# Forgetting attention: where in the unit loop the output projection's weight pieces are split

## The chip, the cores and the metric

The kernel runs on one core of a Trainium2 chip. The metric is the device time of one execution in microseconds (us). TensorE (PE) multiplies matrices, VectorE (DVE) and ScalarE (ACT) work on tiles element by element, GpSimd (POOL) does a smaller share of such work and issues some DMAs, and SyncE (SP) issues most DMAs. Each engine works through its own instructions in the order in which the program hands them out, and instructions of different engines wait for each other through semaphores.

## What is computed

A trunk of two layers over x (1 x 512 x 1024, fp32): a dilated-window attention layer with a gated convolution FFN, then a layer of forgetting attention, which shares one set of keys, values and cumulative gates c, with another FFN. The change lies in the forgetting attention:

```python
def fox_mixer(xn, w_q, w_o, k, v, c):
    q = (xn @ w_q).reshape(B, T, B_HEADS, HEAD_DIM)          # 16 heads of 64
    for i in range(T // BLK):                                # 4 blocks of 128 queries
        s = jnp.einsum('bqhd,bkhd->bhqk', q[:, q0:q1], k[:, :q1]) * scale
        s = s + (c_t[:, :, q0:q1, None] - c_t[:, :, None, :q1])
        p = jax.nn.softmax(jnp.where(causal, s, NEG), axis=-1)
        outs.append(jnp.einsum('bhqk,bkhd->bqhd', p, v[:, :q1]))
    return jnp.concatenate(outs, axis=1).reshape(B, T, B_WIDTH) @ w_o
```

## The kernel before

fp32 products are made of three matmuls. Each operand is split into a high part, rounded to the type that PE reads, and a low part that holds the rest; high by high, high by low and low by high are added up. So every weight is handled in pieces of 128 x 1024 by the class `Weights`, which has three steps for one piece:

- a load from HBM into a raw tile (L50, queue SP), made some pieces ahead: `high` of one piece also loads the piece behind the next one, since `ahead_dma` is 1 in this stage;
- `W.high()`: a copy on ACT that makes the high part (L60);
- `W.low()`: a subtraction on DVE, raw minus high (L78). In another form, `W.minus()` writes the negated and rounded raw tile with ACT (L71) and `W.low_added()` lets a DMA of POOL's queue add the raw tile to the result (L98); that form takes no DVE time.

The attention runs over 32 units (j, i): pair j of heads (0 to 7) and query block i (0 to 3). Unit (j, i) has (i + 1) * 128 keys. The loop hands out, for the unit at hand and its neighbours:

- on DVE `f_exp` (L1640), which adds the bias to the scores and finds the maximum, one instruction for each of two heads, then `f_norm` (L1652), which scales the probabilities of the unit before by the reciprocal of their sum;
- on ACT the exponentials of the unit (L1642), and copies of transposed probabilities out of PSUM (L1666);
- on POOL `f_bias` for the unit behind (L1612 and L1613);
- on PE the transposes of the probabilities of the unit two back (L1664); at i = 2 also the scores (L1630) of two blocks of this pair and two of the next, and the products with the values of the pair before (L1679, tile `o_ps`);
- `q_part` on PE (tile `q_ps`): queries of coming pairs, a quarter to a unit. The results are split by ACT at i = 0 (L1552) and by DVE at i = 1 (L1558).
- `f_out_high` and `f_out_low` (L1689 and L1693): the split of a pair's attention output, tile `OTb`.

The order is written out by hand (`manual_schedule`), so nothing is moved by a planner. All tiles of a kind come from one pool; PSUM has 8 banks, which scores, transposes and sums share.

The weight pieces that this stage splits are those of w_q_b (one for each pair) and then the eight of w_o_b, called wo0 to wo7 here. In pairs 2 to 5 one piece is split in each pair: high at the end of unit (j, 0), then negated and added by DMA at (j, 1). The last of these is wo0, in pair 5. From pair 6 on the DVE form is used, one piece to a unit: the highs of wo1, wo2 and wo3 stand at the end of units (6, 1), (6, 2) and (6, 3), and their lows in units (6, 2), (6, 3) and (7, 0), between `f_bias` and the transposes:

```python
            if i == 2 and j < 2 or (j, i) >= (6, 2):
                W.low()
```

In the last eight steps of the loop (from unit (6, 3) on) PE also gets `po.both(kc, b)`, six instructions of output projection for piece kc = 0 to 3 and row block b = 0, 1 (three for each half of 512 columns; tile `acc`). Behind the loop `po.finish` makes the rest of the first four pieces, and then those of wo4 to wo7; the first of these also splits the four pieces that remain and the first four of the next FFN (eight in a row on ACT and on DVE).

Of the kernel before, what the change touches and what calls it, by code (L numbers as in the profile page):

```python
# [117 lines left out]
def trunk_kernel(ctx, tc, x, norm_gains, w_qkv_a, w_o_a, w_q_b, w_o_b, kv_norm, w_kvf, b_f,  # L118
# [11 lines left out]
    def t8(shape, dt=F32, name="t8"):  # L130
        return p8.tile(shape, dt, tag="t8", name=name)
# [7 lines left out]
    def bank(shape, name="bank"):  # L139
        return psp.tile(shape, F32, tag="ps", name=name)  # L140
# [76 lines left out]
    W = Weights(nc, new_raw, lambda: t8([128, 2, 1024], F32R, name="w"), pieces)  # L217
# [64 lines left out]
    def mm3(o, ah, al, bh, bl, first, last, shared=False):  # L282
        pe.matmul(o, ah, bh, start=first, stop=False, skip_group_check=shared)  # L283
        pe.matmul(o, ah, bl, start=False, stop=False, skip_group_check=shared)  # L284
        pe.matmul(o, al, bh, start=False, stop=last, skip_group_check=shared)  # L285
# [90 lines left out]
    class Proj:  # L376
# [12 lines left out]
        def step(self, kc, b, hf):  # L389
            ah, al = self.get_act(kc)  # L390
            w = self.weight(kc)
            s = slice(b * 128, b * 128 + 128)
            if kc == 0:
                self.banks[b, hf] = bank([128, 512], name="acc")
            mm3(self.banks[b, hf], ah[:, s], al[:, s], w[0][:, H2[hf]], w[1][:, H2[hf]], kc == 0, kc == self.KC - 1)
# [1132 lines left out]
    def load_ck(j):  # L1528
        t = t4([128, 2, T], name="ck")
        s = cd[2 * j:2 * j + 2, :]  # L1530
        sp.dma_start(t, bass.AP(tensor=s.tensor, offset=s.offset, ap=[[0, 128], [T, 2], [1, T]]))
        cks[j] = t
# [4 lines left out]
    def q_part(j, i):  # L1537

        if j >= 8:
            return  # L1540
        if i == 0:
            qps[j] = (bank([128, T], name="q_ps"), [t.rearrange("p (k c) -> p k c", k=8) for t in W.get()])
        o, (wh, wl) = qps[j]
        for kc in (2 * i, 2 * i + 1):
            bh, bl = xs(xTq, kc, ALL)
            mm3(o, wh[:, kc, :], wl[:, kc, :], bh, bl, kc == 0, kc == KD - 1)

    def q_high(j):
        if j >= 8:
            return  # L1550
        qT[j] = t8([128, 2, T], F32R, name="qst")
        act.copy(qT[j][:, 0], qps[j][0])  # L1552

    def q_low(j):
        if j >= 8:
            return
        o, t = qps.pop(j)[0], qT[j]
        dve.tensor_tensor(t[:, 1], o, t[:, 0].bitcast(F32), ALU.subtract)  # L1558
# [48 lines left out]
    def f_bias(j, i):  # L1607
        n = (i + 1) * 128
        bias = t4([128, 2, T], name="bias")
        for hh in range(2):  # L1610
            hd = 2 * j + hh
            pool.tensor_scalar(bias[:, hh, :n], cks[j][:, hh, :n], -1.0, cq[:, i, hd:hd + 1], ALU.mult, ALU.add)  # L1612
        pool.affine_select(bias[:, :, n - 128:n], bias[:, :, n - 128:n], pattern=[[0, 2], [-1, 128]],  # L1613
                           compare_op=ALU.is_ge, fill=NEG, base=0, channel_multiplier=1)
        bia[j, i] = bias
# [3 lines left out]
    def f_scores(j, blocks):  # L1619
        wide = blocks[0] >= 2  # L1620
        if not wide:
            both = [bank([128, 2, 256], name="s_ps") for _ in range(2)]
        k = kst[j // 2][:, j % 2]
        for i in blocks:
            nn = max(256, (i + 1) * 128)
            sc[j, i] = [bank([128, T], name="s_ps") for _ in range(2)] if wide else [o[:, i] for o in both]
            for qp, kp in ((0, 0), (0, 1), (1, 0)):
                for hh in range(2):
                    own = slice(64 * hh, 64 * hh + 64)
                    pe.matmul(sc[j, i][hh][:, :nn], qT[j][own, qp, i * 128:(i + 1) * 128], k[own, kp, :nn],  # L1630
                              start=qp + kp == 0, stop=qp == 1)

    def f_exp(j, i):
        n = (i + 1) * 128
        s = sc.pop((j, i))
        bias = bia.pop((j, i))
        p = t4([128, 2, T], name="prob")
        nm, ls = small(2, "nm"), small(2, "ls")
        for hh in range(2):
            dve.tensor_tensor_reduce(p[:, hh, :n], s[hh][:, :n], bias[:, hh, :n], -0.125, BIG, ALU.add, ALU.min,  # L1640
                                     nm[:, hh:hh + 1])
            act.activation(p[:, hh, :n], p[:, hh, :n], AF.Exp, bias=nm[:, hh:hh + 1], scale=-1.0,  # L1642
                           accum_out=ls[:, hh:hh + 1])
        prob[j, i] = (p, ls)

    def f_norm(j, i):
        n = (i + 1) * 128
        p, ls = prob[j, i]
        rl = small(2, "rl")
        dve.reciprocal(rl, ls)  # L1650
        for hh in range(2):
            dve.tensor_scalar(p[:, hh, :n], p[:, hh, :n], rl[:, hh:hh + 1], None, ALU.mult)  # L1652
# [3 lines left out]
    def f_transpose(j, i):  # L1656
        p, _ = prob.pop((j, i))
        for hh in range(2):
            if i >= 2 or hh == 0:
                o = bank([128, 4, 128], name="pT_ps")  # L1660
                t = t2([128, 4, 128], name="pT")
            k0 = (i + 1) * hh if i < 2 else 0
            for k in range(i + 1):
                pe.transpose(o[:, k0 + k, :], p[:, hh, k * 128:(k + 1) * 128], ident)  # L1664
            if i >= 2 or hh == 1:
                act.copy(t[:, :k0 + i + 1], o[:, :k0 + i + 1])  # L1666
            pT[j, i, hh] = t[:, k0:k0 + i + 1]
# [16 lines left out]
    def f_out_high(j):  # L1684
        o = ops[j]
        if j % 2 == 0:
            OTb[j // 2] = t8([128, 2, 2, T], F32R, name=f"OTb{j // 2}")
        t = OTb[j // 2]
        act.copy(t[:, 0, j % 2, :], o)  # L1689

    def f_out_low(j):
        o, t = ops.pop(j), OTb[j // 2]
        dve.tensor_tensor(t[:, 1, j % 2, :], o, t[:, 0, j % 2, :].bitcast(F32), ALU.subtract)  # L1693

    units = [(j, i) for j in range(8) for i in range(4)]
    po = Proj(8, 4, lambda kc: (OTb[kc // 2][:, 0, kc % 2, :], OTb[kc // 2][:, 1, kc % 2, :]))
    wo = W.n_get + 7
    fill = [(kc, b) for b in range(2) for kc in range(4)]
    W.ahead, W.ahead_dma = 1, 1
    for i in range(3):  # L1700
# [9 lines left out]
    def values_of(n):  # L1710
        nonlocal pv_next
        while pv_next < n - 2:
            j, i = units[pv_next]
            pv_next += 1
            f_pv(j, i)
            if i == 3:
                outs.append(j)

    f_scores(0, (0, 1))
    for n in range(N + 3):  # L1720
        live = n < N
        if live:
            j, i = units[n]
            if i == 0 and j + 1 < 8:
                load_ck(j + 1)
            if i == 2:
                q_part(j + 2, 1)
                f_scores(j, (2, 3))
                if j + 1 < 8:
                    f_scores(j + 1, (0, 1))  # L1730
                values_of(n)
        if live:
            f_exp(j, i)
        if 1 <= n <= N:
            f_norm(*units[n - 1])
        if live:
            if n + 1 < N:
                f_bias(*units[n + 1])
            if i == 1:
                q_low(j + 1)  # L1740
            if i == 2 and j < 2 or (j, i) >= (6, 2):
                W.low()
            if i == 3 and j:
                f_out_low(j - 1)
            if i != 2:
                q_part(j + 1 + (i > 0), (i + 3) % 4)
            if (j, i) in ((7, 1), (7, 2)):
                next(down1)
        if 2 <= n < N + 2:
            f_transpose(*units[n - 2])  # L1750
        if live and i == 1 and 2 <= j < 6:
            W.minus()
            W.low_added()
        if n >= N + 3 - len(fill):
            po.both(*fill[n - N - 3 + len(fill)])

        if n >= N and n % 4 in (0, 2):
            values_of(n)
        while outs:
            f_out_high(outs.pop())  # L1760
        if live and i == 0:
            q_high(j + 1)
        if live and (i == (j < 2) if j < 6 else (j, i) >= (6, 1) and W.n_split < wo + 4):
            W.high()

    for _ in range(2):
        next(down1)
# [50 lines left out]
```

## Time and profile before

| | |
|---|---|
| median of 3 runs | 1107.76 us (1107.25 to 1108.35) |
| the profiled execution: its time | 1107.3 us |
| its span in the trace | 1105.5 us |
| granted TensorE clock | 0.999 |
| the stretch of the unit loop that is changed | about 686 to 726 us |

Times in the views are microseconds from the start of the span. A row of a timeline has the start, the duration, the engine, the line of the kernel, the operation, what it writes and reads, how many equal instructions are merged in the row, and in square brackets the idle time before it with what ended it. Where rows are merged the duration goes from the first start to the last end. PE's ends are modelled: matmuls overlap, and the step from one start to the next tells how fast they go.

### The profile page before, as it was taken

How to read it: one execution, taken by the hardware profiler on the slowest of the kernel's cores; microseconds unless marked ns; L12 is line 12 of the kernel's file. 1: busy time of each engine (PE TensorE's matmuls, PEld its weight loads, DVE VectorE, ACT ScalarE, POOL GpSimd, SP SyncE). 2: the span in 40 equal slices, each digit the busy share in tenths (PEclk: the TensorE clock that was granted, in tenths of full speed). 3: DMA queues.
4: the chain of work that ended last, by engine and by line, in shares of the span. 5: the costliest groups of instructions: out<-in, count | busy, mean ns of one | idle time of the engine just before them, and what ended most of it. 6: DMA issues, size and time to landing. Idle time of an engine off the chain costs nothing.

```text
span 1105.5 us, 18058 instructions
## 1 busy us (share of the span) xinstructions
PE 1095.3 (99%) x6609; PEld 951.4 (86%) x6609; DVE 878.3 (79%) x1493; ACT 672.3 (61%) x1116; POOL 213.3 (19%) x309
## 2 busy tenths in 40 slices
PE   9999999999999999999999999999999999999997
PEld 6988889899999988888878788789899999988886
DVE  6697788888788689897686677868888788779894
ACT  7654575756666747576451587746656666647572
POOL 2632001311111211000000546500311111211000
PEclk9999999999999999999999999999999999999999
DMA  9799854477987989794447434684368878979862
GB/s 323 179 367 411 312 170 136 90 184 187 214 191 185 243 264 324 287 322 116 133 153 274 172 108 123 187 267 128 84 179 202 203 186 186 235 265 325 311 248 76
DMA packets 184928, 236.26 MB, mean 214 GB/s; under 512 B 12352, under 2 KB 132152, under 8 KB 184840
## 3 DMA queue, kind: packets, MB, share of 16 engines
q1 hardware_dynamic: 169224, 182.94, 50.9%
q0 software_dynamic: 14944, 52.18, 20.6%
q8 instruction: 52, 0.85, 0.3%
q14 instruction: 36, 0.29, 0.1%
q10 hardware_dynamic: 672, 0.00, 0.0%
HBM read 166.08 MB, written 39.63 MB: 186 GB/s over the span
## 4 chain that ended last, share of the span: by engine, by line
PE 94%; ACT 2%; DVE 1%; DMA 1%; issue 1%; POOL 0%; SPq 0%; DVEq 0%; ACTq 0%; POOLq 0%
PE up L284 13%; PE up L283 13%; PE up L285 13%; PE acc L283 9%; PE acc L285 8%; PE acc L284 8%; PE v_ps L283 2%; PE v_ps L285 2%; PE v_ps L284 2%; PE qk_ps L284 2%; PE qk_ps L283 2%; PE qk_ps L285 2%; PE first L285 1%; PE first L283 1%; PE first L284 1%; PE k_ps L285 1%
## 5 line engine op out<-in xcount | busy, mean ns | idle before, releaser
L283 PE MATMUL acc<-w 128*128 128x512 f32 (+1 forms) x311 | 120.6, 388 | 0.3 <-DVE mix L332 0.3
L285 PE MATMUL acc<-w 128*128 128x512 f32 (+1 forms) x311 | 120.4, 387 | 0.0
L284 PE MATMUL acc<-w 128*128 128x512 f32 (+1 forms) x267 | 103.2, 387 | 0.0
L283 PE MATMUL up<-xsh,w 128*128 128x256 f32 x352 | 99.6, 283 | 0.0
L284 PE MATMUL up<-xsl,w 128*128 128x256 f32 x352 | 99.6, 283 | 0.0
L285 PE MATMUL up<-xsh,w 128*128 128x256 f32 x352 | 99.6, 283 | 0.0
L78 DVE TENSOR_TENSOR w<-wraw,w 128x1024 fp32r<-128x1024 f32 x62 | 82.0, 1339 | 21.6 <-ACT w L60 21.2
L620 ACT ACTIVATE bb<-up,conv 128x512 f32<-128x512 f32 x80 | 59.6, 776 | 58.7 <-DVE up L1007 47.9
L60 ACT CAST w<-wraw 128x1024 fp32r<-128x1024 f32 x82 | 84.3, 1048 | 17.1 <-PE v_ps L284 6.9
L284 PE MATMUL up<-xcl,w 128*128 128x512 f32 (+1 forms) x276 | 93.5, 339 | 0.0
L284 PE MATMUL up<-xbl,w 128*128 128x512 f32 (+1 forms) x276 | 93.5, 339 | 0.0
L283 PE MATMUL up<-xbh,w 128*128 128x512 f32 (+1 forms) x276 | 93.5, 339 | 0.0
L283 PE MATMUL up<-xch,w 128*128 128x512 f32 (+1 forms) x276 | 93.5, 339 | 0.0
L285 PE MATMUL up<-xbh,w 128*128 128x512 f32 (+1 forms) x276 | 93.5, 339 | 0.0
L285 PE MATMUL up<-xch,w 128*128 128x512 f32 (+1 forms) x276 | 93.4, 338 | 0.0
L283 PEld LDWEIGHTS acc<-w 128*128 128x128 f32 x311 | 58.4, 188 | 12.4 <-DVE mix L332 0.7
L285 PEld LDWEIGHTS acc<-w 128*128 128x128 f32 x311 | 58.4, 188 | 12.0
L283 PEld LDWEIGHTS up<-xsh,w 128*128 128x128 f32 x352 | 67.6, 192 | 0.0
L284 PEld LDWEIGHTS up<-xsl,w 128*128 128x128 f32 x352 | 67.6, 192 | 0.0
L285 PEld LDWEIGHTS up<-xsh,w 128*128 128x128 f32 x352 | 67.6, 192 | 0.0
L621 DVE SCALAR_TENSOR_TENSOR bb<-up,conv,bb 128x511 f32<-128x511 f32 x80 | 59.5, 743 | 5.5 <-ACT bb L620 5.5
L623 DVE SCALAR_TENSOR_TENSOR bb<-up,conv,bb 128x510 f32<-128x510 f32 x80 | 59.9, 748 | 2.8
(312 smaller groups left out, 3154.8 us busy)
## 6 DMA issues: line engine op xcount, KB each, us to landing
wraw<-in_w_up_dram SPq DMA_DIRECT2D x88, 512.0 KB, 5.7
w<-wraw POOLq DMA_DIRECT2D x32, 512.0 KB, 6.4
dT<-dsums SPq DMA_DIRECT2D x28, 512.0 KB, 6.6
w<-wsum POOLq DMA_DIRECT2D x24, 512.0 KB, 5.8
dsums<-in_w_down_dram SPq DMA_DIRECT2D x22, 512.0 KB, 7.5
dsums<-in_w_down_dram SPq DMA_DIRECT2D x44, 256.0 KB, 7.5
hD<-hc POOLq DMA_DIRECT2D x44, 256.0 KB, 6.4
dact<-hD SPq DMA_DIRECT2D x44, 256.0 KB, 5.4
```

The costliest lines, as they stand in the source:

```text
L60: self.nc.scalar.copy(pair[:, 0], raw)
L78: self.nc.vector.tensor_tensor(pair[:, 1], raw, pair[:, 0].bitcast(F32), ALU.subtract)
L283: pe.matmul(o, ah, bh, start=first, stop=False, skip_group_check=shared)
L284: pe.matmul(o, ah, bl, start=False, stop=False, skip_group_check=shared)
L285: pe.matmul(o, al, bh, start=False, stop=last, skip_group_check=shared)
L620: act.activation(bb[:, s, :], ps, AF.Identity, bias=cp[:, 3, ch:ch + 1], scale=cp[:, 2, ch:ch + 1])
L621: dve.scalar_tensor_tensor(bb[:, s, 1:], ps[:, :T - 1], cp[:, 1, ch:ch + 1], bb[:, s, 1:], ALU.mult, ALU.add)
L623: dve.scalar_tensor_tensor(bb[:, s, 2:], ps[:, :T - 2], cp[:, 0, ch:ch + 1], bb[:, s, 2:], ALU.mult, ALU.add)
```

## The change

The low of units (6, 2) and later in the middle of the loop body goes, and so does the rule that puts highs at the end of units from (6, 1) on. In their place a table names, for five units, steps at the very end of the loop body (behind `f_transpose`, `po.both`, `f_out_high` and `q_high`): wo1 is split at the end of (5, 1), behind the minus and the added DMA of wo0; the high of wo2 at the end of (6, 0), its low at the end of (6, 1) with high and low of wo3; wo4's high at the end of (7, 0) and its low at the end of (7, 1). One piece more, wo4, is split inside the loop, and one fewer behind it. Each high still issues one load on SP, so the loads move with the highs.

```diff
-    wo = W.n_get + 7
+    out_weights = {(5, 1): (W.high, W.low), (6, 0): (W.high,), (6, 1): (W.low, W.high, W.low), (7, 0): (W.high,),
+                   (7, 1): (W.low,)}
...
-            if i == 2 and j < 2 or (j, i) >= (6, 2):
+            if i == 2 and j < 2:
                 W.low()
...
-        if live and (i == (j < 2) if j < 6 else (j, i) >= (6, 1) and W.n_split < wo + 4):
+        if live and j < 6 and i == (j < 2):
             W.high()
+        if live:
+            for step in out_weights.get((j, i), ()):
+                step()
```

The order of instructions on each engine: on PE nothing moves. On DVE the subtractions of wo1 to wo3 go from behind the norms of (6, 1), (6, 2) and (6, 3) to in front of `f_exp` of (5, 2) (one) and of (6, 2) (two), and that of wo4 in front of `f_exp` of (7, 2). On ACT the copies go behind L71 of pair 5 (wo1), behind the query copy L1552 of (6, 0) (wo2), behind the copies of the transposes of (5, 3) (wo3, in the place where wo1 was) and behind those of (6, 2) (wo4).

## The prediction

> **What bounds the kernel now.** I read the busy shares first, then the windows around the unit loop's end, then PE's waits, then the timelines engine by engine.
>
> ```profile
> PE 1095.3 (99%) x6609; PEld 951.4 (86%) x6609; DVE 878.3 (79%) x1493; ACT 672.3 (61%) x1116; POOL 213.3 (19%) x309
> ```
>
> PE is busy 99% of the span, so time can come only from PE's few idle stretches, and a step moved elsewhere costs only what PE then waits for. The windows (start:end, length, then busy time and count of PE, PEld, DVE, ACT, POOL, then clock, DMA share, GB/s) show where those stretches are:
>
> ```profile
> 686.00:698.00 12.00, 11.96 (x112) 9.81 (x111) 9.16 (x30) 9.70 (x28) 8.37 (x15) 1.00 0.54 135
> 698.00:711.00 13.00, 11.61 (x106) 9.23 (x102) 11.80 (x34) 10.66 (x28) 9.74 (x14) 1.00 0.70 241
> 711.00:726.00 15.00, 15.00 (x139) 12.21 (x135) 10.70 (x26) 6.71 (x17) 2.22 (x4) 1.00 0.65 217
> 726.00:740.00 14.00, 14.00 (x62) 11.62 (x63) 9.26 (x10) 8.29 (x10) 0.00 (x0) 1.00 1.14 325
> ```
>
> Between 698 and 711 PE lacks 13.00 - 11.61 = 1.39 us; it lacks nothing from 711 to 740. The clock is 1.00 throughout. Of PE's waits over the whole span one group is of this place, and the timeline shows its largest, at (6,3)'s transposes:
>
> ```profile
> PE pT_ps L1664 <- DVE prob L1652: 1.4, 3, 1.1
> ...
> 701.65 0.88 PE L1664 MATMUL pT_ps<-ident,prob 128*128 128x128 f32 x6
> 703.75 0.82 PE L1664 MATMUL pT_ps<-ident,prob 128*128 128x128 f32 x6
> 707.03 0.66 PE L1664 MATMUL pT_ps<-ident,prob 128*128 128x128 f32 x4 [1.07 <-DVE prob L1652]
> 707.96 0.63 PE L1664 MATMUL pT_ps<-ident,prob 128*128 128x128 f32 x4 [0.27 <-ACT pT L1666]
> ```
>
> The transposes of a unit wait for DVE's norm (L1652) of that unit. From 698 to 711 DVE is busy 11.80 of 13.00 us, so DVE sets the pace there, just, and PE stands 1.07 and 0.27 us. This decides the case: lows on DVE are moved earlier, to (5,1) and (6,1), and the question is whether PE has work ahead while DVE does them.
>
> **The change part by part.** PE's instructions keep their order. "Late" below is against the traced execution.
>
> *wo1 at the end of (5,1).* Its high goes on ACT behind wo0's negated copy, its low on DVE ahead of `f_exp` of (5,2).
>
> ```profile
> 687.20 1.08 ACT L71 ACTIVATE w<-wraw 128x1024 fp32r<-128x1024 f32 x1
> 688.25 0.62 ACT L1642 ACTIVATE prob<-prob,nm 128x384 f32<-128x384 f32 x1
> 697.59 1.07 ACT L1666 COPY pT<-pT_ps 128x512 f32<-128x512 f32 x2
> 698.53 1.07 ACT L60 CAST w<-wraw 128x1024 fp32r<-128x1024 f32 x1
> 699.48 0.64 ACT L1642 ACTIVATE prob<-prob,nm 128x384 f32<-128x384 f32 x1
> ```
>
> ACT starts the negated copy (L71) at 687.20 and the next instruction 1.05 later. A high (L60) lasts 1.07 and takes 0.95 from start to next start (698.53 to 699.48). So wo1's high runs from about 688.2 to 689.25, and its low can't start before 689.25. DVE's rows here (L1640 is `f_exp`, first of two heads; L1652 is `f_norm`; L78 a low):
>
> ```profile
> 687.65 0.56 DVE L1640 CUSTOM_DVE_ANT_0 prob<-s_ps,bias 128x384 f32<-128x384 f32 x1 [2.08 <-PE s_ps L1630]
> 688.80 1.55 DVE L1652 TENSOR_SCALAR prob<-prob,rl 128x256 f32<-128x256 f32 x2
> 691.39 0.69 DVE L1640 CUSTOM_DVE_ANT_0 prob<-s_ps,bias 128x512 f32<-128x512 f32 x1 [1.05 <-POOL bias L1613]
> 694.84 1.28 DVE L1652 TENSOR_SCALAR prob<-prob,rl 128x512 f32<-128x512 f32 x2
> 698.28 0.54 DVE L1640 CUSTOM_DVE_ANT_0 prob<-s_ps,bias 128x384 f32<-128x384 f32 x1
> 699.42 0.66 DVE L1652 TENSOR_SCALAR prob<-prob,rl 128x256 f32<-128x256 f32 x2
> 700.00 1.20 DVE L78 TENSOR_TENSOR w<-wraw,w 128x1024 fp32r<-128x1024 f32 x1
> 701.12 0.68 DVE L1640 CUSTOM_DVE_ANT_0 prob<-s_ps,bias 128x512 f32<-128x512 f32 x1
> 703.96 1.23 DVE L78 TENSOR_TENSOR w<-wraw,w 128x1024 fp32r<-128x1024 f32 x1 [0.45 <-ACT w L60]
> 705.10 0.68 DVE L1693 TENSOR_TENSOR OTb<-o_ps,OTb 128x512 fp32r<-128x512 f32 x1
> 706.32 1.49 DVE L1652 TENSOR_SCALAR prob<-prob,rl 128x512 f32<-128x512 f32 x2
> 707.73 1.21 DVE L78 TENSOR_TENSOR w<-wraw,w 128x1024 fp32r<-128x1024 f32 x1
> ```
>
> A low costs DVE 1.12 (700.00 to the next start at 701.12). What lies beside it on POOL is the bias of (5,3):
>
> ```profile
> 689.19 1.69 POOL L1612 TENSOR_SCALAR bias<-ck,cq 128x512 f32<-128x512 f32 x2
> 696.90 1.46 POOL L1612 TENSOR_SCALAR bias<-ck,cq 128x512 f32<-128x512 f32 x2 [0.52 <-DVE rl L1650]
> 699.41 1.96 POOL L1612 TENSOR_SCALAR bias<-ck,cq 128x128 f32<-128x128 f32 x2 [0.56 <-DVE rl L1650]
> 706.68 2.75 POOL L1612 TENSOR_SCALAR bias<-ck,cq 128x512 f32<-128x512 f32 x2
> ```
>
> Norms and biases stretch each other: two biases of 512 columns took 1.46, 1.69 and 2.75 us, the norm of 256 columns 1.55 beside POOL's row at 689.19 and 0.66 at 699.42. So the bias that starts at 689.19, 0.06 before the low, may hold it off for one of its two instructions, 1.46 / 2 = 0.73. I take that: the low runs from 689.9, and `f_exp` of (5,2) starts at 691.0 in place of 687.65. In a sentence apart: the Trainium skill, "SBUF — State Buffer", section "Who interferes with whom", says of DVE in its two-port modes and GpSimd: "Whoever issues first gets the shared pair for the whole instruction; the other **fully blocks**"; the stretched rows agree that they collide, not that the block is whole, and by it the 0.06 us lead is what makes the difference between this sum and the first rival below.
>
> From `f_exp` to the norm behind it is 688.80 - 687.65 = 1.15; the norm of (5,1) costs 0.66 to 1.55, I take 1.0, as the bias is half done by then. So `f_exp` of (5,3) starts at 691.0 + 1.15 + 1.0 = 693.15, not 691.39: 1.75 late. The 3.35 us are cut to 1.75 by the 1.05 us for which DVE stood ahead of 691.39, and by the shorter norm. From there DVE runs without a gap to the norm of (5,3), whose end moves from 694.84 + 1.28 = 696.12 to 697.87. Who waits for that:
>
> ```profile
> 691.17 0.44 PE L1664 MATMUL pT_ps<-ident,prob 128*128 128x128 f32 x2
> 694.69 2.14 PE L1664 MATMUL pT_ps<-ident,prob 128*128 128x128 f32 x14
> 696.76 2.62 PE L1630 MATMUL s_ps<-kst,qst 64*128 64x384 f32 x24
> ```
>
> The transposes of (5,0) at 691.17 write a PSUM bank that the first scores of (5,2) leave when their `f_exp` has read them, now at 691.0 + 0.56: PE about 0.4 late. In the 14 transposes from 694.69 on, the last four belong to the second half of that norm, and the scores at 696.76 follow 0.64 behind its end: there PE already moves with DVE. So PE is then 1.75 late: a further +1.35.
>
> *wo2's high at (6,0), and low wo2, high and low wo3 at (6,1).* On ACT, wo2's high stands ahead of the exponentials of (6,1): 0.95 more before the copies (L1666) of (5,3)'s transposes. These start at 697.59 + 1.75 + 0.95 = 700.3 and wo3's high 0.94 behind them (698.53 - 697.59), from 701.2 to 702.3. Low wo2, ready long before, is over by then. Low wo3 waits for that high, and behind it on DVE is queued `f_exp` of (6,2), with the norm of (6,1): low wo3 from 702.3 to 703.4, `f_exp` at 703.4 in place of 698.28, norm of (6,1) from 703.4 + (699.42 - 698.28) = 704.55 to 705.2. PE's six transposes at 701.65 hold two of (6,0) and four of (6,1); the last two of these ran at about 702.0 and now wait until 705.2: PE is 3.2 late, +1.45 on the 1.75.
>
> Here too a load moves: wo3's, which SP now issues at (5,1), behind the ck load of pair 7.
>
> ```profile
> 690.91 0.33 SPq L1531 DMA_DIRECT2D ck<-cd  x1
> 694.81 6.75 SPq L50 DMA_DIRECT2D wraw<-in_w_o_b_dram  x3
> ...
> DMA to landing us min/median/max: 3.8/5.9/8.2
> ```
>
> At worst it is issued 1.5 us behind 690.91 (the bias of (5,3), late by one low and its wait, is what the ck load waits for) and lands 8.2 later, at 700.6, ahead of 701.2: no cost, with 0.6 us to spare. wo4's load likewise moves out of the three at 694.81 to earlier, with more to spare.
>
> *What is given back.* In (6,2) and (6,3) DVE no longer has its lows. From 701.12 to the end of the norm of (6,3), 706.32 + 1.49 = 707.81, were 6.69 us; of these low wo2 and its wait, from 703.96 - 0.45 = 703.51 to 705.10, 1.59, are gone. `f_exp` of (6,3) now starts at about 705.15, so that norm ends at 705.15 + 6.69 - 1.59 = 710.25: 2.45 late. PE's last four transposes of (6,3), at 707.96 before, then start at 710.4. PE came to them 3.2 late but loses its two stalls there: net -0.8. PE is 2.4 late, and no wait of PE's follows until 740 in the windows above.
>
> *wo4 in the loop, one piece fewer behind it.* The low that stood at 707.73 goes (-1.12 on DVE) and wo4's is added a unit later (+1.12): PE is full from 711 to 726 and DVE busy 10.70 of 15.00, which hides it; were the cover gone, 1.12. Behind the loop ACT and DVE are spared 0.95 and 1.12, but PE is busy 14.00 of 14.00 there: worth 0.
>
> Sum: 0.4 + 1.35 + 1.45 - 0.8 = **+2.4 us**. The profiled execution took 1107.3 us for a span of 1105.5, so it would take 1109.7; the median of the runs shown is 1107.76, 0.46 above it, and gives **1110.2**. Here 0.2% of the time, about what a measurement of this kernel can tell from no change, is 2.2 us.
>
> **The rivals.**
>
> *The low of wo1 gets in first.* If the low isn't held off (the 0.06 us are less than what my steps are known to), it starts at 689.25, DVE is 1.75 - 0.73 = 1.0 late in (5,3), and all that follows is 0.7 earlier: +1.7, so 1109.5. For it: the lows at 700.00 to 707.73 lasted 1.20 to 1.23 though POOL's rows beside them were stretched to 1.96 and 2.75, so it was POOL that gave way. Against: norms did stretch.
>
> *Not slower: DVE's tail is what bounds, and it is relieved.* The two stalls of (6,3) and their like go, and the steps moved to (5,1) and (6,1) find cover in PE's queue. If all 1.39 us between 698 and 711 go and nothing is added, 1107.76 - 1.39 = 1106.4. It decides at 691.39, where DVE stood 1.05 us idle: if `f_exp` of (5,3) is less than about 0.4 late there, and wo3's high is done before DVE comes to it, this is the outcome. For it: PE's idle time is at the tail alone. Against: L71 and L60 can't be done before 689.25, whatever DVE does. In a sentence apart: the Trainium skill, "Perfetto Trace Analysis", section "Identifying the Most-Contended Engine", has one improve the engine that is most occupied, by which moves on DVE and ACT beside a PE at 99% are worth about nothing, 1107.8; the 1.07 us stall shows that they are not hidden everywhere.
>
> *The port is fought over again at (6,1).* If the delayed norm of (6,1) meets a bias as the norm at 688.80 did, it takes 1.55, not 0.66: 0.9 on top of the chain that ends last, +3.3, so 1111.1. The same side is reached if wo3's load lands late, for each us beyond its 0.6. Against: POOL is busy for 9.74 of the 13.00 us there, so 3.26 are free of it.
>
> That the change doesn't do what it says is excluded by the instruction order: the pieces move to where the table puts them.
>
> **How the numbers follow.** The forecast gets 0.46, the low that gets in first 0.22, the second fight 0.18, not slower 0.14. The forecast's own range, from what the norm of (5,1) costs (0.66 to 1.55 about 1.0: -0.35 and +0.55) and the copies' shift, is 1109.4 to 1111.0. The whole range reaches down to 1106.8, over half of the not-slower case, and up to 1112.4, which leaves out 0.08 where fight and late load come together. Slower by over 2.2 us (above 1109.96): 0.6 of the forecast, 0.28, the second fight 0.18, and 0.02 of the first rival: 0.48. Faster by over 2.2 us needs more than the 1.39 us that PE lacks there: 0.06. The rest, 0.46, is within.
>
> **What would show it.** Right: L60 twice in a row from 687.2, `f_exp` of (5,2) at 691.0 with DVE idle time before its low put down to ACT or POOL; the norm of (5,3) ending near 697.9; new PE waits for DVE at (5,3) and (6,1); PE's stalls of 1.07 and 0.27 gone; the loop ending 2.4 us later. Wrong: `f_exp` of (5,3) within 0.4 us of 691.39; wo3's high before DVE has finished low wo2; or a change of time behind 726, where I have none.

## The result and the profile after

| 21 runs of each | median, us | range |
|---|---|---|
| before | 1107.85 | 1106.77 to 1111.13 |
| after | 1109.31 | 1107.95 to 1111.20 |

The ratio after to before is 1.0013, 95% interval 1.0007 to 1.0019: slower by 1.4 us (0.8 to 2.1). The prediction had +2.4 us; its first rival, in which the low of wo1 gets in first, had +1.7. Among the runs of the experiments further below, one execution of one kernel (lows in both gaps) took 1350.62 us at a granted clock of 0.752; its ratio leaves that one out.

The profiled execution of after took 1109.31 us, with a span of 1107.5. In the page, PE is as busy as before:

```profile
PE 1096.1 (99%) x6609; PEld 951.7 (86%) x6609; DVE 877.2 (79%) x1493; ACT 672.3 (61%) x1116; POOL 212.6 (19%) x309
```

To see where two executions part I matched the 6609 PE instructions of the two traces one by one and took how much later each starts. The median difference is 0.72 us just ahead of the first changed place, 1.41 behind the transposes of (5, 3), 3.39 in the middle of the six of (6, 2) (3.54 behind the last of them), 2.02 behind those of (6, 3), and 2.03 from 740 to 880 us. The first 0.7 us are not the change's: they arise near 387 us, where PE waits 0.8 us for a DMA that the kernel before shows no wait for, long ahead of the first instruction that moves. What the change does is 2.02 - 0.72 = 1.3 us in this pair of traces, in three steps: +0.7 at (5, 3), +2.0 at (6, 1) and (6, 2), -1.4 at (6, 3). PE's waits over the whole span of after (in total, times, longest):

```profile
PE pT_ps L1664 <- DVE prob L1652: 1.6, 3, 1.2
...
PE up L285 <- DMA w<-wsum: 0.8, 1, 0.8
PE pT_ps L1664 <- ACT prob L1642: 0.7, 1, 0.7
```

The same transposes in PE's timeline of after (start, duration, idle time before in brackets; about 0.7 of each start is that earlier offset). PE waits before (5, 3) and inside (6, 1), and the two stalls at (6, 3) are gone:

```profile
691.89 0.44 PE L1664 MATMUL pT_ps<-ident,prob 128*128 128x128 f32 x2
...
695.39 0.82 PE L1664 MATMUL pT_ps<-ident,prob 128*128 128x128 f32 x6
696.95 1.21 PE L1664 MATMUL pT_ps<-ident,prob 128*128 128x128 f32 x8 [0.74 <-ACT prob L1642]
698.10 2.70 PE L1630 MATMUL s_ps<-kst,qst 64*128 64x384 f32 x24
...
704.74 0.93 PE L1664 MATMUL pT_ps<-ident,prob 128*128 128x128 f32 x4 [1.24 <-DVE prob L1652]
...
706.98 1.14 PE L1664 MATMUL pT_ps<-ident,prob 128*128 128x128 f32 x6
...
709.34 1.25 PE L1664 MATMUL pT_ps<-ident,prob 128*128 128x128 f32 x8
```

The view puts the 0.74 us down to ACT's exponentials of (6, 0), which end at 696.91; the first half of DVE's norm of (5, 3) had ended only 0.1 us before. Both stand behind the late `f_exp` of (5, 3) on DVE.

DVE's rows at the two changed places, with ACT's highs and POOL's bias beside them:

```profile
687.87 1.08 ACT L71 ACTIVATE w<-wraw 128x1024 fp32r<-128x1024 f32 x1
688.83 1.05 ACT L60 CAST w<-wraw 128x1024 fp32r<-128x1024 f32 x1
...
700.91 1.06 ACT L60 CAST w<-wraw 128x1024 fp32r<-128x1024 f32 x1
```

```profile
689.91 1.23 DVE L78 TENSOR_TENSOR w<-wraw,w 128x1024 fp32r<-128x1024 f32 x1 [3.67 <-ACT w L60]
691.06 0.55 DVE L1640 CUSTOM_DVE_ANT_0 prob<-s_ps,bias 128x384 f32<-128x384 f32 x1
...
692.21 0.76 DVE L1652 TENSOR_SCALAR prob<-prob,rl 128x256 f32<-128x256 f32 x2
692.89 0.68 DVE L1640 CUSTOM_DVE_ANT_0 prob<-s_ps,bias 128x512 f32<-128x512 f32 x1
...
696.32 1.14 DVE L1652 TENSOR_SCALAR prob<-prob,rl 128x512 f32<-128x512 f32 x2
...
699.69 1.21 DVE L78 TENSOR_TENSOR w<-wraw,w 128x1024 fp32r<-128x1024 f32 x1
702.01 1.23 DVE L78 TENSOR_TENSOR w<-wraw,w 128x1024 fp32r<-128x1024 f32 x1 [1.11 <-ACT w L60]
703.15 0.55 DVE L1640 CUSTOM_DVE_ANT_0 prob<-s_ps,bias 128x384 f32<-128x384 f32 x1
...
704.30 0.88 DVE L1652 TENSOR_SCALAR prob<-prob,rl 128x256 f32<-128x256 f32 x2
705.10 0.67 DVE L1640 CUSTOM_DVE_ANT_0 prob<-s_ps,bias 128x512 f32<-128x512 f32 x1
...
708.63 1.24 DVE L1652 TENSOR_SCALAR prob<-prob,rl 128x512 f32<-128x512 f32 x2
```

```profile
689.87 2.47 POOL L1612 TENSOR_SCALAR bias<-ck,cq 128x512 f32<-128x512 f32 x2
```

At (5, 1), L60 starts 0.96 behind L71 and ends at 689.88; the low starts at 689.91, at once, and DVE's next instruction 1.15 later. So the low was not held off; POOL's two biases beside it took 2.47 us. At (6, 1) the second low waits 1.11 us for L60, and `f_exp` of (6, 2) stands behind it until 703.15, 2.3 us longer than behind the first low alone (699.69 and 1.15 for a low).

### The profile page after: what moved, and what is told of

It is laid out like the page before. It is cut to its first block, busy times and chain, and to the rows that moved or that the text cites. A ratio compares the mean times of both kernels' runs of the same rounds, so it can differ in the third digit from the quotient of the medians.

```text
span 1107.5 us, 18060 instructions
## 1 busy us (share of the span) xinstructions
PE 1096.1 (99%) x6609; PEld 951.7 (86%) x6609; DVE 877.2 (79%) x1493; ACT 672.3 (61%) x1116; POOL 212.6 (19%) x309
## 4 chain that ended last, share of the span: by engine, by line
PE 93%; DVE 2%; ACT 1%; DMA 1%; issue 1%; POOL 0%; DVEq 0%; ACTq 0%; POOLq 0%
PE up L285 12%; PE up L283 12%; PE up L284 12%; PE acc L283 9%; PE acc L285 8%; PE acc L284 8%; PE v_ps L283 2%; PE v_ps L285 2%; PE v_ps L284 2%; PE qk_ps L284 2%; PE qk_ps L285 2%; PE qk_ps L283 2%; PE first L285 1%; PE first L283 1%; PE first L284 1%; PE k_ps L285 1%
## 5 line engine op out<-in xcount | busy, mean ns | idle before, releaser
L60 ACT CAST w<-wraw 128x1024 fp32r<-128x1024 f32 x82 | 84.4, 1048 | 16.3 <-PE v_ps L284 6.9
```

Of the source, the lines that this page charges most:

```text
L60: self.nc.scalar.copy(pair[:, 0], raw)
```

## The experiments

All kernels were timed in several rounds on the same chip as runs of the kernel before. The intervals of their ratios are about 0.09% to each side, 1 us, as wide as what is looked for; so each profile was also matched with the trace of before, PE instruction by PE instruction. Differences in us, by place: (5, 3) is read behind the scores that follow its transposes, (6, 2) in the middle of its six transposes (behind the last of them a loss is 0.15 to 0.2 larger, and so is what (6, 3) then gives back), the last behind 712 us; "timed" is the ratio times 1107.8:

| kernel | (5, 3) | (6, 1), (6, 2) | (6, 3) | sum | ratio (95%) | timed |
|---|---|---|---|---|---|---|
| the change | +0.69 | +1.98 | -1.38 | +1.29 | 1.0013 (1.0007 to 1.0019) | +1.4 |
| first part | +0.71 | 0.00 | 0.00 | +0.72 | 1.0012 (1.0004 to 1.0021) | +1.3 |
| second part | +0.05 | +2.02 | -1.38 | +0.69 | 1.0002 (0.9993 to 1.0010) | +0.2 |
| wo1's low in (5, 2) | +0.56 | +2.03 | -1.39 | +1.19 | 1.0009 (1.0000 to 1.0018) | +1.0 |
| wo4 only | +0.18 | 0.00 | -0.41 | -0.23 | 0.9998 (0.9990 to 1.0007) | -0.2 |
| wo3's low in (6, 2) | +1.66 | +0.79 | -0.97 | +1.48 | 1.0007 (0.9998 to 1.0016) | +0.8 |
| one low behind norm (6, 3) | +0.30 | 0.00 | -0.73 | -0.43 | 0.9994 (0.9985 to 1.0003) | -0.7 |
| wo0's low in the gap | -0.74 | 0.00 | -0.67 | -1.41 | 0.9983 (0.9974 to 0.9992) | -1.9 |
| lows in both gaps | -0.71 | 0.00 | -1.52 | -2.22 | 0.9976 (0.9967 to 0.9985) | -2.7 |
| before, added DMA moved | +0.81 | 0.00 | +0.03 | +0.85 | 1.0005 (0.9996 to 1.0014) | +0.6 |
| change, added DMA moved | +0.37 | +1.96 | -1.38 | +0.95 | 1.0007 (0.9998 to 1.0016) | +0.8 |
| change, wo0 by DVE | +0.63 | +1.98 | -1.38 | +1.24 | 1.0008 (0.9999 to 1.0017) | +0.9 |

Where nothing was changed ahead of a place, the column shows how much one execution differs from another: up to 0.3 at (5, 3), 0.4 at (6, 3). In no kernel did PE's difference change by more than 0.05 between 712 and 880 us, so up to there none lost or won anything behind the loop. From 888 us on it grows by 0.1 to 0.4 us in four of them (in three at a wait for a weight DMA); the sums leave that out, and the changed kernel doesn't have it.

In the diffs below `out_weights` is the table of steps at the end of a unit. A second table stands in the old place of the lows, in the middle of the unit; it is added in all but the two kernels that move the added DMA:

```diff
-            if i == 2 and j < 2:
+            if i == 2 and j < 2 or (j, i) in out_lows:
                 W.low()
```

**The first part alone** (against the kernel after):

```diff
+    out_weights = {(5, 1): (W.high, W.low), (6, 2): (W.high,), (6, 3): (W.high,)}
+    out_lows = ((6, 3), (7, 0))
```

> Only the first part of the change: wo1 is split at the end of (5, 1), wo2 and wo3 keep the places that they had (highs at the end of (6, 2) and (6, 3), lows in (6, 3) and (7, 0)), and wo4 stays behind the loop. Theory (late norms: each moved low holds up the softmax of the next unit, and PE pays where it has nothing queued): PE is 0.8 us late from the transposes of (5, 3) on, as in the changed kernel; the low that is gone from (6, 2) gives nothing back, since the low in (6, 3) waits for its high on ACT instead (that wait grows from 0.45 to about 1.5 us), so +0.8 at the end, 1108.6. Rival (occupied DVE: a low costs 1.12 us of a DVE that paces PE from 698 to 711, wherever it stands): +0.8 at (5, 3), but the stall of 1.07 at (6, 3) goes, so -0.3, 1107.6. Rival (loads and pieces: the loss comes from wo4 and the moved loads): 0.0.

+0.7 at (5, 3), and nothing given back, as the first theory had it. DVE's rows show why one low less in (6, 2) is worth nothing: DVE reaches the next low early and waits for its high.

```profile
689.14 1.23 DVE L78 TENSOR_TENSOR w<-wraw,w 128x1024 fp32r<-128x1024 f32 x1 [3.68 <-ACT w L60]
...
704.76 1.23 DVE L78 TENSOR_TENSOR w<-wraw,w 128x1024 fp32r<-128x1024 f32 x1 [1.85 <-ACT w L60]
...
707.11 1.49 DVE L1652 TENSOR_SCALAR prob<-prob,rl 128x512 f32<-128x512 f32 x2
```

The wait was 0.45 before and is 1.85 here; the norm of (6, 3) starts 0.79 later than before (707.11 against 706.32), by PE's own lateness. Occupied DVE, as the rival had it, is refuted: a low less, and the time is no better (the interval, +0.4 to +2.3, leaves out its -0.3).

**The second part alone:**

```diff
+    out_weights = {(6, 0): (W.high,), (6, 1): (W.low, W.high, W.low), (7, 0): (W.high,), (7, 1): (W.low,)}
+    out_lows = ()
```

> Only the second part: wo1 in place of wo2 in the steps of (6, 0) and (6, 1) (high; low, high, low with wo2), wo3 in place of wo4 at (7, 0) and (7, 1); nothing is split at (5, 1). Theory (late norms): 0 at (5, 3), PE late by about 1.7 to 2.1 us at (6, 1) and (6, 2), 1.3 to 1.5 given back at (6, 3): +0.6, 1108.4. With the first part's +0.8 that makes the +1.4 of the whole change. Rival (occupied DVE): as many lows before (6, 3)'s norm as in the kernel before, and none later, so about 0. Rival (loads and pieces): 0.0, as wo4 stays behind the loop.

By place +0.05, +2.02, -1.38: in the trace the two parts add up to the whole within 0.12 (0.72 + 0.69 against 1.29). The timed +0.2, with an interval from -0.8 to +1.1, is below that and holds it; by time alone the rivals' 0 stands as well, by place they don't.

**wo1's low in DVE's idle time of (5, 2):**

```diff
+    out_weights = {(5, 1): (W.high,), (6, 0): (W.high,), (6, 1): (W.low, W.high, W.low), (7, 0): (W.high,),
+                   (7, 1): (W.low,)}
+    out_lows = ((5, 2),)
```

> The changed kernel with the low of wo1 handed out in the middle of unit (5, 2), behind the norm of (5, 1), instead of at the end of (5, 1); its high stays. Theory (late norms): DVE stood 1.05 us idle at that place in the kernel before, so the low fits; 0.1 instead of 0.8 us late at (5, 3), the second part's +0.6 stays: +0.7, 1108.5. POOL's bias of (5, 3) is then half done, and the norm of (5, 1) goes back to its 1.55 us beside it. Rival (occupied DVE): the same low in the same stretch, +1.4, 1109.2.

The theory's 0.1 at (5, 3) did not come; it was +0.56. DVE and POOL here:

```profile
688.63 1.31 DVE L1652 TENSOR_SCALAR prob<-prob,rl 128x256 f32<-128x256 f32 x2
689.86 1.69 DVE L78 TENSOR_TENSOR w<-wraw,w 128x1024 fp32r<-128x1024 f32 x1
691.85 0.69 DVE L1640 CUSTOM_DVE_ANT_0 prob<-s_ps,bias 128x512 f32<-128x512 f32 x1 [0.30 <-POOL bias L1613]
```

```profile
688.78 1.69 POOL L1612 TENSOR_SCALAR bias<-ck,cq 128x512 f32<-128x512 f32 x2
690.54 1.28 POOL L1613 TENSOR_SCALAR_AFFINE_SELECT bias<-bias 128x256 f32<-128x256 f32 x1
```

The low took 1.69 in place of 1.23, and POOL's last step for the bias of (5, 3) (L1613) 1.28 in place of 0.41: it ends at 691.82, when `f_exp` starts. DVE's idle time there was time in which POOL worked for it, so a low in it takes from the very thing that DVE waits for. In the changed kernel POOL alone gave way (its first bias took 1.80 us, its second 0.73); here both did. The Trainium skill, "SBUF — State Buffer", section "Who interferes with whom", has the port pair as an exclusive lock that goes to the one that issues first, and counts a DVE instruction with two inputs in SBUF, which the low is, among those that contend with POOL's reads. These rows agree with it to 0.15 us, if a row's start is the issue and not the taking of the lock: the low spans what was left of the biases (to 690.47) and its own 1.2, and L1613 spans what was left of the low (to 691.55) and its own 0.4. In the changed kernel POOL's row starts 0.04 us ahead of the low and yet gave way, so the starts don't tell who came first at that distance.

**wo4 alone** (against the kernel before):

```diff
+    out_weights = {(6, 1): (W.high,), (6, 2): (W.high,), (6, 3): (W.high,), (7, 0): (W.high,)}
+    out_lows = ((6, 2), (6, 3), (7, 0), (7, 1))
```

> The kernel before with one piece more inside the loop: wo4's high at the end of (7, 0), its low in (7, 1); one fewer behind the loop. Both theories of DVE: PE is full from 711 on, 0.0 us (within 0.2). Rival (loads and pieces: what is split behind the loop matters, or wo5's load going ahead of the loads of the FFN's sums delays these): beyond 0.3 us either way, with a step of PE's shift behind 711.

Timed -0.2 with zero well inside, and no step behind 711. The -0.41 at (6, 3) goes with a norm of (6, 3) that took 1.03 in this execution, not 1.49; the change comes behind that norm, so this is the spread of that place. A piece more in the loop and one fewer behind it cost nothing that shows.

**wo3's low behind the norm of (6, 1):**

```diff
+    out_weights = {(5, 1): (W.high, W.low), (6, 0): (W.high,), (6, 1): (W.low, W.high), (7, 0): (W.high,), (7, 1): (W.low,)}
+    out_lows = ((6, 2),)
```

> The changed kernel with the low of wo3 handed out in the middle of unit (6, 2), behind the norm of (6, 1), instead of at the end of (6, 1); its high stays at the end of (6, 1). The same lows, in the same stretch, but f_exp of (6, 2) no longer stands behind a low that waits for ACT. Theory (the wait for the high is the larger part of the loss at (6, 1)): DVE's 1.11 us of waiting there go, f_exp of (6, 2) comes about 2.3 us earlier, PE's wait of 1.24 at (6, 1) goes, the rest is late by one low only: +0.4 on the kernel before in place of +1.4, 1108.1. Rival (occupied DVE: the lows' 1.12 us each are what counts): +1.4, 1109.1.

At (6, 1) and (6, 2) the loss fell from 1.98 to 0.79 with as many lows in the stretch; with (6, 3) the second part is worth -0.18 in place of +0.60, 0.8 better, where the theory had 1.0. PE waits 0.2 us at a time there, and `f_exp` of (6, 2) stands behind one low, not behind two and a wait:

```profile
701.62 1.21 DVE L78 TENSOR_TENSOR w<-wraw,w 128x1024 fp32r<-128x1024 f32 x1
702.75 0.55 DVE L1640 CUSTOM_DVE_ANT_0 prob<-s_ps,bias 128x384 f32<-128x384 f32 x1
...
704.62 1.21 DVE L78 TENSOR_TENSOR w<-wraw,w 128x1024 fp32r<-128x1024 f32 x1
```

The sum can't be read from this trace: at (5, 3) it lost 1.66 us. In this execution ACT was already 0.95 us later against PE when it came to (5, 1), ahead of all that was moved: L71 starts 1.41 us behind the scores of (5, 2), 0.46 in the trace of after. With that lateness PE does wait at the transposes of (5, 0), for the bank that `f_exp` of (5, 2) frees, as the prediction had it:

```profile
693.59 0.44 PE L1664 MATMUL pT_ps<-ident,prob 128*128 128x128 f32 x2 [0.66 <-DVE nm L1640]
```

Timed, the kernel was at +0.8, between the theory's +0.4 and the rival's +1.4; the interval holds both. The wait for the high is the larger part of the loss at (6, 1) by place; by time it is not settled.

**One low behind the norm of (6, 3)** (against the kernel before):

```diff
+    out_weights = {(6, 1): (W.high,), (6, 2): (W.high,), (7, 0): (W.high,)}
+    out_lows = ((6, 2), (7, 0), (7, 1))
```

> The kernel before with wo2's low in unit (7, 0), behind the norm of (6, 3), instead of in (6, 3) ahead of it; wo3's high then goes to the end of (7, 0) and its low to (7, 1). Theory (what a low costs is set by the norm that it stands ahead of, and PE waits only for the norm of (6, 3)): the low and its wait, 1.59 us, are gone ahead of that norm, which then waits for the exponentials of (6, 3) on ACT, so that it ends 1.1 us earlier; PE's stalls of 1.07 and 0.27 shrink to 0.2: -1.1, 1106.5. Rival (PE is full at 99% and the stall moves on): wo2 is now late for the output projection, which wants it at 708.8, and the time goes there: 0.0.

-0.73 at (6, 3), -0.7 timed, against -1.1 forecast; the interval (-1.7 to +0.3) holds zero. That norm now waits for ACT, and some of the gain is lost 1 us later, where PE wants wo2 (the step by step difference goes from -1.41 to -0.94 there):

```profile
705.17 0.17 DVE L1650 RECIPROCAL rl<-ls 128x2 f32<-128x2 f32 x1 [0.94 <-ACT prob L1642]
705.37 1.03 DVE L1652 TENSOR_SCALAR prob<-prob,rl 128x512 f32<-128x512 f32 x2
706.32 1.21 DVE L78 TENSOR_TENSOR w<-wraw,w 128x1024 fp32r<-128x1024 f32 x1
```

**wo0 finished by DVE in the gap of (5, 1)** (the added steps, against the kernel after):

```diff
-        if live and i == 1 and 2 <= j < 6:
+        if live and i == 1 and 2 <= j < 5:
             W.minus()
             W.low_added()
...
+    out_weights = {(5, 1): (W.low, W.high), (6, 2): (W.high,), (7, 0): (W.high,), (7, 1): (W.high,)}
+    out_lows = ((6, 2), (7, 0), (7, 1), (7, 2))
```

> Both ideas in one: wo0 is finished by DVE at the end of (5, 1), in the 2.1 us for which DVE stood idle ahead of f_exp of (5, 2) in the kernel before, so its negated copy on ACT and its added DMA on POOL go and wo1's high takes the copy's place; wo1's low is in (6, 2) as before, then wo2: high at the end of (6, 2), low in (7, 0); wo3: high (7, 0), low (7, 1); wo4: high (7, 1), low (7, 2). Theory: 0 or up to -0.4 at (5, 3), since the bias of (5, 3) no longer stands behind the DMA's issue on POOL, and -1.1 at (6, 3): -1.3, 1106.3. Rival (a low hurts wherever it is): +0.8 at (5, 3), -0.3 in all.

-0.74 at (5, 3), where the forecast had 0 to -0.4, and -0.67 at (6, 3) for its -1.1; timed -1.9 (-2.9 to -0.9), faster than before. In the 2.08 us in which DVE waited for PE's scores a low cost nothing that shows: it took 1.55 us beside a bias of POOL, and DVE still waited 0.39 us for the scores behind it.

**Lows in both gaps:** the same, with

```diff
+    out_weights = {(5, 1): (W.low, W.high), (6, 1): (W.high,), (6, 3): (W.high,), (7, 0): (W.high,)}
+    out_lows = ((5, 2), (6, 3), (7, 0), (7, 1))
```

> As the run before it, but wo1's low goes to the middle of (5, 2), DVE's second idle gap, and the rest one place forward: wo2's high at the end of (6, 1), its low in (6, 3), wo3's high at the end of (6, 3), its low in (7, 0), wo4's high at the end of (7, 0), its low in (7, 1). Theory: the low in (5, 2) runs beside POOL's bias of (5, 3) and makes it late, as in the run where wo1's low stood there (+0.55), less the 0.4 by which the bias starts earlier: +0.2 at (5, 3); DVE then has one low less before the norm of (6, 3) and no wait for a high: -1.3 there, -1.1 in all, 1106.5. Rival (port): the full +0.55, -0.8 in all.

Better than both theories: 1105.25 us, 0.9976 (0.9967 to 0.9985) of before, 4 us under the changed kernel's 1109.31 by the medians. The windows (686 to 698, 698 to 711; PE's busy time is the number behind the length) show PE without idle time at (5, 3) and nearly without in the tail:

```profile
686.00:698.00 12.00, 12.00 (x122) 10.24 (x121) 11.47 (x35) 10.29 (x30) 8.51 (x15) 1.00 0.30 92
698.00:711.00 13.00, 12.86 (x137) 10.86 (x133) 12.82 (x38) 11.80 (x31) 8.08 (x12) 1.00 0.70 243
```

A part of the gain was never idle time in PE's own rows. It stood in PEld, PE's weight loads, in the kernel before:

```profile
695.51 0.42 PEld L1664 LDWEIGHTS pT_ps<-ident,prob 128*128 128x128 f32 x4 [0.24 <-ACT prob L1642]
696.18 0.42 PEld L1664 LDWEIGHTS pT_ps<-ident,prob 128*128 128x128 f32 x4 [0.24 <-DVE prob L1652]
698.41 0.77 PEld L1630 LDWEIGHTS s_ps<-kst,qst 64*128 64x128 f32 x11 [0.36 <-DVE qst L1558]
```

At these three places PE's difference falls by 0.20, 0.26 and 0.25, and all three waits are gone.

In the second gap POOL no longer worked on what DVE waits for. Without the added DMA of wo0, POOL's bias of (5, 3) started 3.7 us earlier against PE's work and was done before the low began:

```profile
685.70 1.26 DVE L78 TENSOR_TENSOR w<-wraw,w 128x1024 fp32r<-128x1024 f32 x1
...
689.27 1.21 DVE L78 TENSOR_TENSOR w<-wraw,w 128x1024 fp32r<-128x1024 f32 x1
690.40 0.68 DVE L1640 CUSTOM_DVE_ANT_0 prob<-s_ps,bias 128x512 f32<-128x512 f32 x1
```

```profile
685.19 2.33 POOL L1612 TENSOR_SCALAR bias<-ck,cq 128x512 f32<-128x512 f32 x2 [0.36 <-PE pT_ps L1664]
687.60 0.41 POOL L1613 TENSOR_SCALAR_AFFINE_SELECT bias<-bias 128x256 f32<-128x256 f32 x1
```

Before, that bias stood on POOL behind the issue of the added DMA, which waits for ACT's L71:

```profile
688.57 0.88 POOL L98 DMA_DIRECT2D w<-wraw  x1 [3.95 <-ACT w L71]
```

The next two runs were to isolate this.

**The added DMA moved behind the bias** (against the kernel before):

```diff
+            if (j, i) == (5, 2):
+                W.low_added()
...
             W.minus()
-            W.low_added()
+            if j < 5:
+                W.low_added()
```

> The kernel before with one step moved: the added DMA of wo0 (L98, queue of POOL) is handed out in unit (5, 2) behind the bias of (5, 3), instead of at the end of (5, 1) ahead of it. Nothing else changes. Theory (POOL stands at that DMA until ACT has written the negated copy, 3.95 us in the trace of before, and the bias queued behind it is what f_exp of (5, 3) waits for, 1.05 us): the bias is done before DVE wants it, and PE's hidden wait at the transposes of (5, 3) goes, as where wo0 was finished by DVE: -0.65 there, nothing at (6, 3), 1107.1. Rival (in that run the gain at (5, 3) came from ACT, which had one copy less): 0.0.

Not the forecast -0.65, since the move made a new wait. The bias of (5, 3) came early (`f_exp` of (5, 3) right behind the norm, at 690.54, with no wait). But POOL's bias of (6, 1) now waits for the landing of that DMA, DVE for the bias, and PE, for the first time, in the scores:

```profile
696.73 0.94 POOL L1612 TENSOR_SCALAR bias<-ck,cq 128x256 f32<-128x256 f32 x2 [5.09 <-DMA w<-wraw]
```

```profile
698.18 0.43 DVE L1640 CUSTOM_DVE_ANT_0 prob<-s_ps,bias 128x256 f32<-128x256 f32 x1 [2.15 <-POOL bias L1613]
```

```profile
698.67 2.52 PE L1630 MATMUL s_ps<-kst,qst 64*128 64x384 f32 x23 [0.93 <-DVE nm L1640]
```

Ahead of that wait PE's difference had fallen by 0.45 at the transposes of (5, 3) (0.99 to 0.54), as much as in the two kernels without that DMA (0.46 in each), though ACT here still makes the copy that it is spared there. So up to this place the gain came from POOL, and ACT's copy isn't needed for it. The other 0.25 to 0.3 of those two arises in the scores behind, where this run lost 1.3 by its new wait; for that part it decides nothing.

**The same move in the changed kernel:** wo0 counts as done at (5, 1), and only its DMA is issued later.

```diff
+            if (j, i) == (5, 2):
+                nc.gpsimd.dma_start(pair[:, 1], raw, accum_op=ALU.add)
```

> The changed kernel with the same single move: the added DMA of wo0 behind the bias of (5, 3). Theory (with the low of wo1 in front of f_exp of (5, 2) DVE is late by itself, whatever POOL does): the norm of (5, 1) is 0.1 to 0.2 us shorter without the bias beside it, no more; +1.2, 1109.0. Rival (the bias is what holds (5, 3) in the changed kernel too): +0.8 less 0.65 and the hidden wait that went in the run before it: 0.0 at (5, 3), +0.6 in all, 1108.4.

+0.37 in place of +0.69 at (5, 3), +0.95 in all, timed +0.8: between the theory (+1.2) and the rival (+0.6). POOL's bias was done by 686.84, 4.6 us before `f_exp` of (5, 3), and DVE was late all the same, behind the low that waited 3.68 us for its high:

```profile
688.63 1.24 DVE L78 TENSOR_TENSOR w<-wraw,w 128x1024 fp32r<-128x1024 f32 x1 [3.68 <-ACT w L60]
...
691.48 0.68 DVE L1640 CUSTOM_DVE_ANT_0 prob<-s_ps,bias 128x512 f32<-128x512 f32 x1
```

So at (5, 3) the change loses by its low; what the bias adds is about 0.3 us, no more than the spread of that place. The run before it bears this out: with the DMA behind the bias, PE's difference at the last transposes of (5, 3) fell by 0.45 without the change's steps and rose by 0.29 with them.

**The change with wo0 by DVE** (with `2 <= j < 5` at the minus and the added DMA, as two runs above):

```diff
+    out_weights = {(5, 1): (W.low, W.high, W.low), (6, 0): (W.high,), (6, 1): (W.low, W.high, W.low), (7, 0): (W.high,),
+                   (7, 1): (W.low,)}
```

> The changed kernel with wo0 finished by a low on DVE at the end of (5, 1) in place of the negated copy and the added DMA; wo1's high and low follow it there, and the rest is as in the change. Theory (the low of wo1 is late since its high stands on ACT behind the negated copy): the high starts one step of ACT, 0.96 us, earlier, the low and f_exp of (5, 2) with it, and the hidden wait at (5, 3) shrinks: -0.2 instead of +0.8 there, the second part's +0.6 stays: +0.4, 1108.2. Rival (occupied DVE: a second low in that place costs another 1.12): +1.4 or more.

Timed +0.9, interval -0.1 to +1.9, which holds the theory's +0.4 and the rival's +1.4. The trace doesn't decide either: as in the run of wo3's low, ACT came to (5, 1) about 0.95 late against PE, and wo1's high started 1.42 us behind the scores of that unit, just as in the changed kernel, with L71 gone. Open.

## Why the prediction was right, and where it wasn't

The sign, the place and the mechanism held: slower by 1.4, within the range, by two new waits of PE for the softmax behind moved lows, with some given back at (6, 3). The size was the first rival's (1109.5) rather than the forecast's: 1109.31 lies just under the forecast's own 1109.4 to 1111.0, and a loss of 1.4 falls among the outcomes within 2.2 us, which the prediction gave 0.46, not among the slower ones, which it gave 0.48. That the sum is no further off than its first two terms (1.06 in the traces) is luck: the misses at (6, 1) with (6, 2) (+0.5) and at (6, 3) (-0.6) cancel. By its steps:

- **The low of wo1 held off by POOL, 0.73:** wrong. It started 0.03 us behind its high. That was the first rival's condition, which this pair of traces bears out at (5, 3): `f_exp` of (5, 3) 0.79 late (692.89 less the earlier offset of 0.71, against 691.39), where the rival had 1.0 and the forecast 1.75. The rest of that is the norm of (5, 1), 0.68 from start to start for the 1.0 that I took. `f_exp` of (5, 2) at 691.06 looks like the forecast's 691.0; less the offset it is 690.35, about where the rival puts it (690.27). The trace of before already had a row against the 0.73: beside the norm of 0.66 at 699.42, which the prediction shows as an unstretched one, POOL's row of 1.96 starts at 699.41, so there, too, it was POOL that gave way.
- **PE 0.4 late at the transposes of (5, 0), for a PSUM bank:** didn't happen: they stand at 691.17 and 691.89, just the offset. It hung on the late low; the trace with ACT 0.95 us late, above, shows the wait.
- **+1.35 more at (5, 3):** +0.69 in all there, and +0.71 in the first part alone, against 1.75. This term, mis-sized by the 0.73 above and by the norm's 0.3, is together with the 0.4 the whole of the miss, as the two terms below cancel.
- **+1.45 at (6, 1):** the chain L60, low wo3, `f_exp`, norm was as written, with DVE's wait of 1.11 for the high; it measured +1.98, 2.02 in the second part alone. The norm of (6, 1) took 0.88, not the 1.55 of the rival in which the port is fought over again. What was missed is (6, 2): I followed PE from (6, 1) straight to (6, 3), but the norm of (6, 2) was late too, and PE lost 0.4 in its six transposes.
- **-0.8 at (6, 3):** -1.38. The norm of (6, 3) took 1.24, not the 1.49 that I carried over, and started 0.8 earlier than forecast, about the 0.73 for which the low of wo1 was not held off.
- **Nothing from 711 on, nothing for wo4:** held; at most 0.05 by place between 712 and 880 us in every kernel.
- **The bound of the gain:** the not-slower rival's best, -1.39, was set by what PE lacks between 698 and 711. The kernel with lows in both gaps gained 2.2 by place, since 0.7 of it were waits of PE's weight loads that don't count as idle time of PE: 0.46 in the row of 14 transposes, which I had read as DVE's pace and not as a wait that can go, and 0.25 in the scores at 698.41.

## What to carry to other kernels

Cost a moved step by what is queued behind it on its engine and by when its own input is ready, not by its duration: a low put right behind its high waits for it, and everything behind the low waits too (the low and its wait held `f_exp` back by 2.3 us at (6, 1)), while a low in idle time that ended on PE's scores cost nothing that shows. Before filling an engine's idle time, read what ends it: time that ended on PE's scores was free here; time that ended on POOL's bias wasn't while POOL still worked on that bias, as the low stretched POOL's last step from 0.41 to 1.28 us. Look also at what a DMA's issue waits for: POOL stood 3.95 us at one that waited for ACT, with its own compute queued behind. And look for waits in PE's weight loads, not in its matmul rows alone.

## What I had not expected

- POOL stood 3.95 us at the issue of an added DMA in the kernel before, and the bias behind it was late for that. With the DMA gone PE's hidden 0.7 us at (5, 3) were gone as well (-0.74 and -0.71 in two kernels). ACT had one copy less there too; the run with only the DMA moved shows the first 0.45 without that, and leaves the rest open.
- One execution differs from another ahead of anything that was edited: near 387 us PE waited for a DMA for 0.8 us (in the changed kernel), 0.9 and 1.0 (in two others), 0.2, or not at all, and at (5, 1) ACT was in two kernels 0.95 us later against PE, for a reason that stays open. Matching the instructions of two traces tells such an offset from what an edit does; the medians alone don't. Each kernel was matched in one execution only, so differences of 0.3 at (5, 3) and 0.4 at (6, 3) mean nothing.
